# Where the split weights of a transformer block lie against the moving operands, and GpSimd's share of the gate and up projections on VectorE

## The chip, the cores and the metric

One core of a Trainium2 chip runs the whole kernel. The metric is the device time of one execution in microseconds. The kernel before was timed in three runs; their median is 2808.41 us (2807.86 to 2812.64). A further execution was taken under the profiler, and all rows of the trace are from that one.

## The reference

One encoder layer over 512 tokens of width 2048, in fp32: two attention mixers whose outputs are gated and merged, then a SwiGLU block of width 5632. What the change touches stands in the last lines:

```python
merged = jax.nn.sigmoid(ga) * (ya @ w_oa[l]) + jax.nn.sigmoid(gb) * (yb @ w_ob[l])
x = x + g1 * (merged @ w_out[l])

h2 = rms_norm(x, norm2_w[l]) * (1.0 + sc2) + sh2
ff = (jax.nn.silu(h2 @ w_ffn_gate[l]) * (h2 @ w_ffn_up[l])) @ w_ffn_down[l]
x = x + g2 * ff
return rms_norm(x, final_w)
```

## The kernel before, in words

**Three matmuls for one.** TensorE gets every fp32 operand as a pair: `split` (L113 to L115) copies a source to a high part on ACT (L114) and subtracts that from the source to a low part, on DVE unless told otherwise (L115). `mm3` (L122 to L124) then issues three matmuls into one bank: high by high, and the two mixed products. In `mm3(o, lh, ll, rh, rl)` the first pair is stationary (loaded as weights), the second pair moves past it.

**Tiles of split weights.** `wsplit` loads 512 KB of a weight matrix into a `raw` tile (DMA issued on SP) and splits it into a `whi` and a `wlo` tile, which `wtile` hands out. From `w_out` on, the pool has five buffers of each; each buffer has 1024 elements and 64 more, so that a tile can begin up to 63 elements (of 4 bytes) into its buffer. Where it begins is `wbufs["at"]` at the moment of the call. All buffers, and all tiles of split activations (`x`, `f`, `m`), begin at multiples of 256 bytes, and columns are taken from them in steps of 512 bytes; so `at` alone sets how a stationary and a moving operand lie against each other within 256 bytes.

**w_out.** `form2` keeps the activations stationary (`m`) and moves the weights, 512 columns a matmul, through four banks for the four blocks of 128 tokens; it is called for columns 0, 1, 2 with `at` 28, 44, 12, and for the last 512 columns in two halves, still at 12. Generators that compute the modulation vectors run between its steps (`pump`). After that `at` is 0.

**Gate and up.** `h2_unit` makes the normalised activations transposed, and `xforms` splits them into tiles `x0` to `x3` of each of four units of 512 rows. The first 512 columns of gate (n = 0) are computed plainly while these are made: weights stationary, 256 columns moving, one of the four moving blocks (`h21`) being itself a `wtile`. Everything else goes through `group7`, one call for up of n = 0 and then one each for gate and up of n = 1 to 10: 21 calls. It uses a Strassen-like scheme with seven products (forms 1, 2, 3, 5, 6, 7, 4, in this order) in place of eight, and takes four units of 84 matmuls each, all with weights stationary and 256 columns moving. For each unit `wforms` loads two raw tiles, forms two sums in `ta` on DVE (L705, L706) and two in `tb` on GpSimd (L707, L708), and splits four sources: a block of 512, a raw tile, `ta` and `tb`. At the end of a call seven operations (L765 to L771) combine the banks on DVE; the banks of forms 1, 2, 3, 5 are the four `mm` banks, which the next call overwrites in the same order. Before each call `at` takes the next value of `at7`: 4, 8, 12, 16, 20 and so on by fours to 60, then 0, 1, 2, 56, 24, 40.

**The product and down.** After up of each n, gate times up is formed (L840), on GpSimd but for the last n, and stored to DRAM (`ffd`). Down reads these back: `FF` loads half a stored tile (1024 wide, `ffr`), and splits it into `f0`, `f1` and so on, the first time a column pass asks for it; these tiles lie where the `x` tiles were. `form2` runs for four column blocks over the first five n and four over the next five (`at` 4, 8, 16, 24 and 32, 40, 48, 60), 240 matmuls of 512 columns in each, with `f` stationary and the weights moving. The last n stays in a tail with its own weight tiles, which begin at multiples of 256 bytes.

**Order.** The program is recorded in the order of the Python code, with some blocks at high priority, and a scheduler places each engine's instructions by priority; the engines execute them in that order and wait by semaphores.

Of the kernel before, what the change touches and what calls it, by code (L numbers as in the profile page):

```python
# [80 lines left out]
def encoder_block(ctx: ExitStack, tc, xp, c, w_ada, b_ada, norm1_w, w_in, q_norm_w, k_norm_w, tb,  # L81
                  w_oa, w_ob, w_out, norm2_w, w_gate, w_up, w_down, final_w, rope, wmask, out):
    nc = tc.nc
    V, S, G = nc.vector, nc.scalar, nc.gpsimd
# [9 lines left out]
    wbufs = {"raw": 4, "w": 3, "pad": 0, "at": 0}  # L94

    def wtile(tag):
        at = wbufs["at"]
        return wp.tile([P, 1024 + wbufs["pad"]], F32R, tag=tag, name=tag, bufs=wbufs["w"])[:, at:at + 1024]
    dram = ctx.enter_context(tc.tile_pool(name="dram", bufs=1, space=bass.MemoryType.DRAM))

    def bank(tag):
        return ps.tile([P, 512], F32, tag=tag, name=tag, bufs={"mm": 4, "S": 2, "T": 1, "Y": 1}[tag])
# [10 lines left out]
    def split(hi, lo, src, eng=V):  # L113
        S.activation(hi, src, AF.Copy)  # L114
        eng.tensor_sub(lo, src, hi)  # L115
# [10 lines left out]
    def unit(w, k0, nk, c0, ncol):  # L126
        raw = wp.tile([P, 1024], F32, tag="raw", name="raw", bufs=wbufs["raw"])
        r3 = raw[:, :nk * ncol].rearrange("p (k n) -> p k n", k=nk)
        nc.sync.dma_start(r3, w[k0 * P:(k0 + nk) * P, c0:c0 + ncol].rearrange("(k p) n -> p k n", p=P))
        return raw[:, :nk * ncol], r3  # L130
# [215 lines left out]
    for n, (k0, k1) in enumerate(slices):  # L346
# [9 lines left out]
        for k in ks:  # L356
            for i in range(NT):
                sl = slice(i * P, (i + 1) * P)
                nc.tensor.matmul(kv_b[i], hT[k][0][:, sl], hi[:, k - k0], start=k == 0, stop=False)
                nc.tensor.matmul(kv_b[i], hT[k][0][:, sl], lo[:, k - k0], start=False, stop=False)  # L360
        for k in ks:
            for i in range(NT):
                sl = slice(i * P, (i + 1) * P)
# [6 lines left out]
        for c0, accs, ends in ((QA, q_acc, (0, 1, 2, 4, 8, 12, 16)), (GA, g_acc, (0, 2, 6, 10, 14, 16))):  # L370
# [8 lines left out]
            for i, acc in enumerate(accs):  # L379
                sl = slice(i * P, (i + 1) * P)  # L380
# [270 lines left out]
        return evac  # L651

    for cc in range(3):
        wbufs["at"] = (28, 44, 12)[cc]
        form2(w_out, cc * 512, mT, residual(cc, gate, sq2, G, x2_d))
    for pr in ((0, 1), (2, 3)):
        form2(w_out, 3 * 512, mT, lambda i, b: residual(3, gate, sq2, V if i % 2 else G, x2_d)(i, b), tiles=pr)
        for i in pr:
# [5 lines left out]
            else:  # L664
                V.tensor_scalar(lo3, lo3, r, None, op0=ALU.mult)
                V.tensor_scalar(n3[i], hi1, r, None, op0=ALU.mult)
    wbufs["at"] = 0
    while bg:
        pump()
    p_m.release()  # L670
# [24 lines left out]
    def wforms(w, k0, c0):  # L695
        rt = []
        for a in range(2):
            raw, r3 = unit(w, k0 + 2 * a, 2, c0, 512)
            rt.append((raw, r3[:, :, :256], r3[:, :, 256:]))
        (_, b11, b12), (r1, b21, b22) = rt  # L700
        ta = wp.tile([P, 1024], F32, tag="ta", name="ta", bufs=2)
        tb = wp.tile([P, 1024], F32, tag="tb", name="tb", bufs=1)
        t1, t2_ = (half(ta)[:, a] for a in range(2))
        t3, t4 = (half(tb)[:, a] for a in range(2))
        V.tensor_sub(t1, b12, b11)  # L705
        V.tensor_sub(t2_, b22, t1)  # L706
        G.tensor_sub(t3, b22, b12)  # L707
        G.tensor_sub(t4, t2_, b21)  # L708
        hl = [[wtile(t) for t in ("whi", "wlo")] for _ in range(4)]
        col = lambda e: lambda t: t.rearrange("p (q n) -> p q n", q=2)[:, :, e * 256:(e + 1) * 256]  # L710
        blk = lambda e: lambda t: half(t)[:, e]
        g0 = [t[:, :512].rearrange("p (q n) -> p q n", q=2) for t in hl[0]]
        return split7(((b11, (lambda t: t,)), (r1, (col(0), col(1))), (ta, (blk(0), blk(1))), (tb, (blk(0), blk(1)))),
                      [g0] + hl[1:], HALVES[0])

    def xforms(pool, e, o, full=False):

        sa = wp.tile([P, 1024], F32, tag="ta", name="sa", bufs=2)
        sb = wp.tile([P, 1024], F32, tag="tb", name="sb", bufs=1)
        a11, a21 = e[:, :512], e[:, 512:]  # L720
        a12, a22 = o[:, :512], o[:, 512:]
        V.tensor_add(sa[:, :512], a21, a22)
        V.tensor_sub(sa[:, 512:], sa[:, :512], a11)
        G.tensor_sub(sb[:, :512], a11, a21)
        G.tensor_sub(sb[:, 512:], a12, sa[:, 512:])
        tl = [[pool.tile([P, 512 if n == 0 else 1024], F32R, tag=f"x{n}{t}", name=f"x{n}{t}") for t in "hl"]
              for n in range(4)]
        blk = lambda n: lambda t: t[:, n * 512:(n + 1) * 512].rearrange("p (q n) -> p q n", q=2)
        d = {}
        if full:  # L730
            h21 = [wtile(t)[:, :512] for t in ("whi", "wlo")]
            split(*tl[0], a11)
            split(*h21, a21)
            split(*tl[1], o)
            d["21"] = tuple(blk(0)(t) for t in h21)
            for n, rs in ((0, (1,)), (1, (2, 4))):
                for j, r in enumerate(rs):
                    d[r] = tuple(blk(j)(t) for t in tl[n])
            d.update(split7(((sa, (blk(0), blk(1))), (sb, (blk(0), blk(1)))), tl[2:], HALVES[1][2:]))
            return d  # L740
        return split7(((a11, (blk(0),)), (o, (blk(0), blk(1))), (sa, (blk(0), blk(1))), (sb, (blk(0), blk(1)))),
                      tl, HALVES[1])

    at7 = iter((4, 8, 12, 16, 20, 24, 28, 32, 36, 40, 44, 48, 52, 56, 60, 0, 1, 2, 56, 24, 40))

    def group7(wsrc, xs, order, dst):

        wbufs["at"] = next(at7)
        bk = {r: bank(BANK[r]) for r in ORDER}
        for n, s in enumerate(order):  # L750
            w = wsrc(s)
            for r in ORDER:
                (wh, wl), (xh, xl) = w[r], xs[s][r]
                for q in range(2):
                    for c in range(2):
                        o = bk[r][:, c * 256:(c + 1) * 256]
                        cs = slice(c * P, (c + 1) * P)
                        first, last = n == 0 and q == 0 and c == 0, n == len(order) - 1 and q == 1
                        mm3(o, wh[:, q, cs], wl[:, q, cs], xh[:, q], xl[:, q], first, last, skip_group_check=True)
        p = {r: b.rearrange("p (c n) -> p c n", c=2) for r, b in bk.items()}  # L760
        (d11, d12), (d21, d22) = dst
        with tc.high_priority():
            p1 = io.tile([P, 512], F32, tag="io", name="p1").rearrange("p (c n) -> p c n", c=2)
            S.activation(p1, p[1], AF.Copy)
            V.tensor_add(d11, p[2], p1)  # L765
            V.tensor_add(d21, p[6], p1)
            V.tensor_add(d12, p[5], d21)
            V.tensor_add(d12, p[3], d12)
            V.tensor_add(d21, p[7], d21)
            V.tensor_add(d22, p[5], d21)  # L770
            V.tensor_sub(d21, d21, p[4])  # L771

    SU = KT // 4
    FU = FT // 4
    f_x = [form_pool(f"f{n}", "left") for n in range(3)]

    def raw_tile(name):
        return wp.tile([P, 1024], F32, tag="raw", name=name, bufs=wbufs["raw"])
# [16 lines left out]
    hx = {}  # L795
    ff_d = [dram.tile([P, 2048], F32, name=f"ffd{n}") for n in range(FU)]
# [24 lines left out]
    def c_tile():  # L821
        c = c_p.tile([P, 2048], F32, tag="c", name="c", bufs=3)
        return c, c.rearrange("p (a t q n) -> p a t q n", a=2, t=2, q=2)

    for n in range(FU):
        cs = []
        for w in (w_gate, w_up):
            c, v = c_tile()
            cs.append(c)
            if n == 0 and w is w_gate:  # L830
                for f in range(4):
                    S.activation(v[:, f // 2, :, f % 2], banks[f].rearrange("p (t n) -> p t n", t=2), AF.Silu)
                continue
            dst = (v[:, 0, 0], v[:, 1, 0]), (v[:, 0, 1], v[:, 1, 1])
            group7(lambda s: wforms(w, 4 * s, n * 512), hx, range(SU), dst)
            if w is w_gate:
                S.activation(c, c, AF.Silu)
        for a in range(2):
            sl = slice(a * 1024, (a + 1) * 1024)
            (G if n < FU - 1 else V).tensor_mul(cs[1][:, sl], cs[1][:, sl], cs[0][:, sl])  # L840
        (nc.sync if n < FU - 1 else nc.scalar).dma_start(ff_d[n], cs[1])
    c_p.release()
    f3.release()
# [27 lines left out]
    class FF:  # L871
# [6 lines left out]

        def __getitem__(self, k):
            j, q = divmod(k, 2)  # L880
            if j not in self.pairs:
                n, a = divmod(j, 2)
                raw = raw_tile("ffr")
                nc.sync.dma_start(raw, ff_d[self.u0 + n][:, a * 1024:(a + 1) * 1024])
                hl = [self.pool.tile([P, 1024], F32R, tag=f"f{j}{t}", name=f"f{j}{t}") for t in "hl"]
                split(*hl, raw)
                self.pairs[j] = hl
            return tuple(Tokens(half(t)[:, :, q]) for t in self.pairs[j])

    for u0 in (0, 5):  # L890
        xs = FF(p_f, u0, 5)
        for cc in range(4):
            wbufs["at"] = (4, 8, 16, 24)[cc] if u0 == 0 else (32, 40, 48, 60)[cc]
            form2(w_down, cc * 512, xs, lambda i, b: residual(cc, g2, None, G)(i, b), r0=4 * u0)
    xs = FF(p_fl, 10, 1)
    xs = [xs[k] for k in range(4)]
# [9 lines left out]
    for cc in range(4):  # L906
        hi, lo = pair(p_l, f"w{cc}", 4 * 512, 1)
        for k in range(0, 4, 2):
            raw, _ = unit(w_down, f0 + k, 2, cc * 512, 512)
            sl = slice(k * 512, (k + 2) * 512)  # L910
            split(hi[:, sl], lo[:, sl], raw)
        wl.append((hi, lo))
    for i in range(NT):
        sl = slice(i * P, (i + 1) * P)
# [8 lines left out]
        for cc in range(4):  # L923
            cs = slice(cc * 512, (cc + 1) * 512)
# [36 lines left out]
```

## Time and profile before

| | us |
|---|---|
| median of 3 runs | 2808.41 |
| span of the profiled execution | 2800.4 |
| w_out | 1175 to 1367 |
| first gate block and its activations | 1367 to 1448 |
| 21 calls of `group7` | 1448.0 to 2281.8 |
| down and the tail | 2289.5 to the end |

The profiled execution has no time of its own beside its span; the runs, taken without the profiler, lie 8.0 us above it. In a row of the view of windows stand the stretch, its length, and each engine's busy time with its count of instructions, then the granted clock of TensorE, the share of the DMA engines and GB/s. PEld is the loading of weights. In a row of the timeline stand start, duration, engine, line, operation, and in brackets the idle time before it and what ended it.

### The profile page before, as it was taken

Reading aid. Unit: us, or ns where it says so; the run is one execution under the profiler, and the core shown is the slowest. Engines: PE = TensorE matmul, PEld = TensorE weight load, DVE = VectorE, ACT = ScalarE, POOL = GpSimd, SP = SyncE. Lnnn points to the kernel's source line nnn. Section 1 sums busy time; section 2 is a strip of 40 time slices with the busy share of each in tenths; the row PEclk is TensorE's granted clock in tenths of the full one; section 3 lists DMA queues with packets and bytes.
Section 4 is the critical chain, followed back from the end, with each engine's and each line's share of the span. In section 5 each row is a group of like instructions: output and inputs, shape, how many; then the busy total and the mean of one; then the engine's idle time right before and its main releaser. Section 6 shows DMA issues by size and latency. Waiting matters only on the chain.

```text
span 2800.4 us, 38853 instructions
## 1 busy us (share of the span) xinstructions
PE 2672.3 (95%) x15353; PEld 2331.3 (83%) x15353; DVE 1730.4 (62%) x2277; ACT 961.7 (34%) x1310; POOL 617.0 (22%) x366
## 2 busy tenths in 40 slices
PE   5888999999999999899899999999999989999998
PEld 4676878788887878677789999999999988878886
DVE  8987461566665566565568877777788753243227
ACT  4224441233331233222544444444444433122122
POOL 2544323000100000011123443333434410011000
PEclk8889999999999999999989999999999999999999
DMA  8772224655556577676333343334333354343232
GB/s 256 255 235 83 83 68 153 193 157 168 173 168 198 186 254 249 221 260 199 95 113 121 122 128 118 116 108 130 126 119 120 125 192 163 97 143 120 90 113 83
DMA packets 281238, 427.17 MB, mean 153 GB/s; under 512 B 16992, under 2 KB 148432, under 8 KB 278496
## 3 DMA queue, kind: packets, MB, share of 16 engines
q1 hardware_dynamic: 280720, 423.59, 46.9%
q8 instruction: 120, 1.97, 0.3%
q10 hardware_dynamic: 336, 1.11, 0.1%
q14 instruction: 62, 0.51, 0.1%
HBM read 392.11 MB, written 32.52 MB: 152 GB/s over the span
## 4 chain that ended last, share of the span: by engine, by line
PE 77%; DVE 10%; DMA 8%; ACT 2%; issue 2%; SPq 0%; POOL 0%; DVEq 0%; ACTq 0%
PE mm L122 19%; PE mm L124 19%; PE mm L123 19%; DMA raw<-in_w_ada 6%; DVE acc L257 5%; PE S L122 3%; PE S L123 3%; PE S L124 3%; PE Y L122 2%; PE Y L123 2%; PE Y L124 2%; DMA ffr<-ffd 1%; ACT whi L114 1%; PE T L494 1%; DVE wlo L115 0%
## 5 line engine op out<-in xcount | busy, mean ns | idle before, releaser
L114 ACT ACTIVATE whi<-raw 128x1024 fp32r<-128x1024 f32 (+1 forms) x466 | 455.2, 978 | 1077.0 <-PE mm L124 404.8
L115 DVE TENSOR_TENSOR wlo<-raw,whi 128x1024 fp32r<-128x1024 f32 (+1 forms) x408 | 499.4, 1227 | 494.6 <-ACT whi L114 489.7
L257 DVE SCALAR_TENSOR_TENSOR acc<-raw,cact,acc 128x512 f32<-128x512 f32 (+1 forms) x383 | 324.9, 851 | 138.0 <-DMA raw<-in_w_ada 129.0
L707 POOL TENSOR_TENSOR tb<-raw 128x512 f32<-128x512 f32 x84 | 116.0, 1380 | 505.6 <-DVE wlo L115 497.8
L115 POOL TENSOR_TENSOR wlo<-raw,whi 128x1024 fp32r<-128x1024 f32 (+1 forms) x58 | 142.7, 2465 | 236.5 <-ACT whi L114 204.9
L115 DVE TENSOR_TENSOR wlo<-ta,whi 128x1024 fp32r<-128x1024 f32 x84 | 129.4, 1541 | 70.5 <-ACT whi L114 70.1
L708 POOL TENSOR_TENSOR tb<-ta,raw 128x512 f32<-128x512 f32 x84 | 145.1, 1727 | 0.0
L646 POOL TENSOR_TENSOR xr<-xr,ro 128x512 f32<-128x512 f32 x32 | 49.3, 1572 | 434.0 <-DVE ro L645 434.0
L114 ACT ACTIVATE whi<-ta 128x1024 fp32r<-128x1024 f32 x84 | 89.2, 1062 | 142.1 <-PE mm L123 142.1
L114 ACT ACTIVATE whi<-tb 128x1024 fp32r<-128x1024 f32 x84 | 89.1, 1061 | 133.4 <-PE S L123 119.9
L123 PE MATMUL mm<-x1l,whi 128*128 128x256 f32 x400 | 112.4, 281 | 0.0
L122 PE MATMUL mm<-x1h,whi 128*128 128x256 f32 x400 | 112.3, 281 | 0.0
L124 PE MATMUL mm<-x1h,wlo 128*128 128x256 f32 x400 | 112.3, 281 | 0.0
L115 DVE TENSOR_TENSOR wlo<-tb,whi 128x1024 fp32r<-128x1024 f32 x84 | 102.5, 1221 | 10.0 <-ACT whi L114 8.3
L122 PE MATMUL mm<-x0h,whi 128*128 128x256 f32 x368 | 104.5, 285 | 3.3 <-ACT whi L114 3.3
L124 PE MATMUL mm<-x0h,wlo 128*128 128x256 f32 x368 | 104.4, 284 | 0.8 <-DVE wlo L115 0.8
L123 PE MATMUL mm<-x0l,whi 128*128 128x256 f32 x368 | 104.5, 284 | 0.0
L250 POOL MEMSET acc<- 128x512 f32 x8 | 4.2, 526 | 427.9 <-DVE ada_s L115 158.6
L123 PE MATMUL mm<-x3l,whi 128*128 128x256 f32 x336 | 94.3, 281 | 0.0
L123 PE MATMUL S<-x2l,whi 128*128 128x256 f32 x336 | 94.3, 281 | 0.0
L123 PE MATMUL S<-x3l,whi 128*128 128x256 f32 x336 | 94.3, 281 | 0.0
L123 PE MATMUL mm<-x2l,whi 128*128 128x256 f32 x336 | 94.3, 281 | 0.0
(1311 smaller groups left out, 8242.9 us busy)
## 6 DMA issues: line engine op xcount, KB each, us to landing
raw<-in_w_in SPq DMA_DIRECT2D x134, 512.0 KB
raw<-in_w_ada SPq DMA_DIRECT2D x256, 256.0 KB
raw<-in_w_gate SPq DMA_DIRECT2D x88, 512.0 KB
raw<-in_w_up SPq DMA_DIRECT2D x88, 512.0 KB
raw<-in_w_down SPq DMA_DIRECT2D x88, 512.0 KB
raw<-in_w_ada SPq DMA_DIRECT2D x64, 512.0 KB
raw<-in_w_out SPq DMA_DIRECT2D x40, 512.0 KB
ffr<-ffd SPq DMA_DIRECT2D x22, 512.0 KB
```

The lines of the kernel that those rows point to most:

```text
L114: S.activation(hi, src, AF.Copy)
L115: eng.tensor_sub(lo, src, hi)
L122: nc.tensor.matmul(o, lh, rh, start=start, stop=False, **kw)
L123: nc.tensor.matmul(o, lh, rl, start=False, stop=False, **kw)
L124: nc.tensor.matmul(o, ll, rh, start=False, stop=stop, **kw)
L250: G.memset(acc, 0.0)
L257: V.scalar_tensor_tensor(acc, part, cact[:, k:k + 1], acc, op0=ALU.mult, op1=ALU.add)
L494: nc.tensor.transpose(tp[:, k * P:(k + 1) * P], e[:, k * P:(k + 1) * P], ident)
L646: eng.tensor_add(x2[i][:, cs], x2[i][:, cs], o)
L707: G.tensor_sub(t3, b22, b12)
L708: G.tensor_sub(t4, t2_, b21)
```

## The change

It does four things. The offsets of `w_out` and of down become 0, and that of all of gate and up 16 elements (64 bytes), with `h21`, which moves, kept at 0. The two `tb` sums of `wforms` and all products of gate and up go from GpSimd to VectorE. During the last unit of the last `group7` call `first_pair` loads and splits the first half tile of `ffd` into a `whi`/`wlo` pair at offset 0, which down takes as its pair 0 in the first half (in `xforms` and the tail nothing else changes).

```diff
     for cc in range(3):
-        wbufs["at"] = (28, 44, 12)[cc]
         form2(w_out, cc * 512, mT, residual(cc, gate, sq2, G, x2_d))
...
-    wbufs["at"] = 0
+    wbufs["at"] = 16
...
-        G.tensor_sub(t3, b22, b12)
-        G.tensor_sub(t4, t2_, b21)
+        V.tensor_sub(t3, b22, b12)
+        V.tensor_sub(t4, t2_, b21)
...
+            at, wbufs["at"] = wbufs["at"], 0
             h21 = [wtile(t)[:, :512] for t in ("whi", "wlo")]
+            wbufs["at"] = at
...
-    at7 = iter((4, 8, 12, 16, 20, 24, 28, 32, 36, 40, 44, 48, 52, 56, 60, 0, 1, 2, 56, 24, 40))
-
     def group7(wsrc, xs, order, dst):
 
-        wbufs["at"] = next(at7)
...
+    pair0 = []
+
+    def first_pair(s):
+        if s == SU - 1:
+            wbufs["at"] = 0
+            raw = raw_tile("ffr")
+            nc.sync.dma_start(raw, ff_d[0][:, :1024])
+            pair0.extend((wtile("whi"), wtile("wlo")))
+            split(*pair0, raw)
+
...
-            group7(lambda s: wforms(w, 4 * s, n * 512), hx, range(SU), dst)
+            src = lambda s: wforms(w, 4 * s, n * 512)
+            if n == FU - 1 and w is w_up:
+                src = lambda s: (wforms(w, 4 * s, n * 512), first_pair(s))[0]
+            group7(src, hx, range(SU), dst)
...
-            (G if n < FU - 1 else V).tensor_mul(cs[1][:, sl], cs[1][:, sl], cs[0][:, sl])
+            V.tensor_mul(cs[1][:, sl], cs[1][:, sl], cs[0][:, sl])
...
         def __getitem__(self, k):
             j, q = divmod(k, 2)
+            if j not in self.pairs and j == self.u0 == 0:
+                self.pairs[0] = pair0
...
         for cc in range(4):
-            wbufs["at"] = (4, 8, 16, 24)[cc] if u0 == 0 else (32, 40, 48, 60)[cc]
```

VectorE at the end of a call of `group7` and the start of the next, before the change (`c` is the call's result, `p` the copied bank of form 1, `mm`, `S` and `Y` are banks; L770 is the last to read form 5's bank):

```order
L766 TENSOR_TENSOR c<-S,p_12008 128x512
L115 TENSOR_TENSOR wlo<-tb,whi 128x1024
L767 TENSOR_TENSOR c<-mm,c 128x512
L768 TENSOR_TENSOR c<-mm,c 128x512
L769 TENSOR_TENSOR c<-S,c 128x512
L115 TENSOR_TENSOR wlo<-raw,whi 128x512
L770 TENSOR_TENSOR c<-mm,c 128x512
L115 TENSOR_TENSOR wlo<-raw,whi 128x1024
L771 TENSOR_TENSOR c<-c,Y 128x512
L115 TENSOR_TENSOR wlo<-ta,whi 128x1024
```

The same place after it, where the lines are two lower (L766 is now L764, L770 is L768) and the call is one of up:

```order
L764 TENSOR_TENSOR c<-S,p_12008 128x512
L115 TENSOR_TENSOR wlo<-tb,whi 128x1024
L765 TENSOR_TENSOR c<-mm,c 128x512
L706 TENSOR_TENSOR tb<-raw 128x512
L766 TENSOR_TENSOR c<-mm,c 128x512
L767 TENSOR_TENSOR c<-S,c 128x512
L707 TENSOR_TENSOR tb<-ta,raw 128x512
L768 TENSOR_TENSOR c<-mm,c 128x512
L115 TENSOR_TENSOR wlo<-raw,whi 128x512
L769 TENSOR_TENSOR c<-c,Y 128x512
L851 TENSOR_TENSOR c<-c 128x1024 x2
L115 TENSOR_TENSOR wlo<-raw,whi 128x1024
```

The two sums of `tb` now stand among the combining operations, ahead of the split that was there, and the product (L851) stands ahead of the next splits.

ACT at the end of the last call and the start of down, before (with buffer numbers; `whi<-raw` are splits of w_down from `whi_21220` on, `p1` is the copy of form 1's bank, `ffd10` the store of the last product):

```order
L114 ACTIVATE whi_21094<-tb_21083 128x1024
L114 ACTIVATE whi_21220<-raw_21218 128x1024
L114 ACTIVATE whi_21269<-raw_21267 128x1024
L764 ACTIVATE p1_21188<-mm_20741 128x512
L114 ACTIVATE whi_21305<-raw_21303 128x1024
L114 ACTIVATE whi_21341<-raw_21339 128x1024
L114 ACTIVATE whi_21377<-raw_21375 128x1024
L841 DMA ffd10_10903<-c_20740 128x2048
L114 ACTIVATE f0h_21226<-ffr_21224 128x1024
L114 ACTIVATE f1h_21275<-ffr_21273 128x1024
```

And after it, where `whi_21106` is `pair0`:

```order
L114 ACTIVATE whi_21094<-tb_21083 128x1024
L114 ACTIVATE whi_21106<-ffr_21104 128x1024
L114 ACTIVATE whi_21226<-raw_21224 128x1024
L762 ACTIVATE p1_21194<-mm_20741 128x512
L114 ACTIVATE whi_21269<-raw_21267 128x1024
L114 ACTIVATE whi_21305<-raw_21303 128x1024
L114 ACTIVATE whi_21341<-raw_21339 128x1024
L114 ACTIVATE whi_21377<-raw_21375 128x1024
L852 DMA ffd10_10903<-c_20740 128x2048
L114 ACTIVATE f1h_21275<-ffr_21273 128x1024
```

The first pair's split has moved from the end of this row of splits to its head, ahead of the five splits of w_down; the others keep their order, and `f1h` follows the fifth.

## The prediction

> **What bounds the kernel now.** First the page: busy shares, then the chain that ended last, by engine.
>
> ```profile
> span 2800.4 us, 38853 instructions
> PE 2672.3 (95%) x15353; PEld 2331.3 (83%) x15353; DVE 1730.4 (62%) x2277; ACT 961.7 (34%) x1310; POOL 617.0 (22%) x366
> PE 77%; DVE 10%; DMA 8%; ACT 2%; issue 2%; SPq 0%; POOL 0%; DVEq 0%; ACTq 0%
> ```
>
> TensorE is busy for 95% of the span and owns 77% of the chain, so what matters is how fast matmuls follow each other and where TensorE stands still. A matmul's own duration in the trace overlaps the next one and does not give the pace. I read the pace from the view of windows, which counts instructions in a stretch: I laid windows on whole calls of `group7`, 336 matmuls of 256 columns each; about two of those counted began before the window.
>
> ```profile
> core 0: us, PE busy (x) PEld busy (x) DVE busy (x) ACT busy (x) POOL busy (x), PEclk, DMA share, GB/s
> 1567.10:1605.20 38.10, 38.10 (x338) 38.10 (x337) 33.97 (x32) 15.81 (x17) 20.04 (x10) 1.00 0.44 139
> 2003.40:2043.70 40.30, 40.30 (x338) 40.30 (x337) 27.96 (x33) 17.55 (x18) 11.62 (x9) 1.00 0.34 105
> 2043.70:2084.00 40.30, 40.30 (x338) 40.30 (x337) 34.50 (x32) 15.74 (x17) 19.11 (x11) 1.00 0.40 131
> 1448.00:2241.60 793.60, 793.60 (x6722) 793.60 (x6722) 618.65 (x617) 332.26 (x351) 309.30 (x179) 1.00 0.38 120
> 2241.60:2281.80 40.20, 40.20 (x337) 40.20 (x336) 23.80 (x27) 17.98 (x18) 8.53 (x6) 1.00 0.37 117
> ```
>
> The work in the first three rows is the same, the granted clock is 1.00 in each, and TensorE never waits; yet the first takes 38.1 us (113.4 ns a matmul) and the others 40.3 (119.9). What differs is the entry of `at7`: the fourth call, the first row, has 16 elements (64 bytes); the fifteenth and sixteenth have 60 and 0. All 20 calls of the fourth row average 39.7 us (118.1 ns). So the address of the weights against the moving operand sets the pace, and this kernel has already run the value that the change gives to every call.
>
> **The change part by part.**
>
> *Calls of `group7`.* At 38.1 us each, 20 calls take 762.0 in place of 793.6, the last one 38.1 in place of 40.2: **33.7 us** gone. I take the fourth call as the rule, not as luck: its DVE and POOL had as much to do as the others'. The ends: 38.1 for all (33.7), or for none but the one, with the rest at their mean now (0).
>
> *512-column matmuls.* For offset 0 with 512 columns I looked for a stretch where no call shifts the tiles: `w_oa`/`w_ob`, ahead of `w_out`, the first row here. The last four are `w_out`'s columns, and down's two halves stand between; the row at 1429 is the first gate block.
>
> ```profile
> 1000.00:1050.00 50.00, 50.00 (x222) 1.00 0.78 250
> 1193.00:1229.70 36.70, 36.70 (x160) 1.00 0.84 290
> 1234.00:1275.80 41.80, 41.80 (x180) 1.00 0.65 210
> 1280.00:1322.30 42.30, 42.30 (x183) 1.00 0.64 199
> 1322.50:1367.20 44.70, 44.70 (x194) 1.00 0.48 153
> 1429.00:1445.00 16.00, 16.00 (x136) 1.00 0.51 164
> 2296.00:2515.00 219.00, 219.00 (x946) 1.00 0.45 152
> 2517.70:2741.60 223.90, 223.90 (x957) 1.00 0.32 104
> 2757.00:2788.00 31.00, 31.00 (x139) 1.00 0.27 94
> ```
>
> (Read by their times: four rows from 1193 are `w_out`, 2296 and 2517 down, 2757 the tail, whose weights lie at 0 with the same stationary `f` tiles as down.) With two taken off each count, the first row has 50.0/220 = 227 ns and the tail 31.0/137 = 226; `w_out` has 232 to 235, down 232 and 234. At 227, `w_out`'s 158+178+181+192 = 709 matmuls take 161.0 in place of 165.5: **4.5 us**. Down's 944 + 955 take 431.1 in place of 442.9: **11.8 us**. The lower end for both is 0, if offset 0 helps only where weights are not the moving operand; the tail's row speaks against that, and against a loss. In `w_out` DMA is up to 0.84 busy, but inside these windows TensorE never waits for a load, so a 2% faster TensorE is still fed.
>
> *First gate block.* 384 matmuls of 256 columns go from offset 0 to 64 bytes; `h21`, moved there, stays at 0. 16.0/134 = 119 ns to 113.4 would give 2.3; part of the block waits for transposes and runs at half clock, so **2.0** (0 to 2.3).
>
> *Start of down.* Here TensorE waits, by the timeline (start, duration, engine):
>
> ```profile
> 2281.81 0.28 PE L124 MATMUL Y<-x1h,wlo 128*128 128x256 f32 x1
> 2289.53 0.79 PE L122 MATMUL mm<-whi,f0h 128*128 128x512 f32 x1 [7.44 <-ACT f0h L114]
> 2295.93 0.40 PE L124 MATMUL mm<-whi,f0l 128*128 128x512 f32 x1
> 2286.74 1.06 ACT L114 ACTIVATE whi<-raw 128x1024 fp32r<-128x1024 f32 x1 [5.00 <-DMA raw<-in_w_down]
> 2288.42 1.06 ACT L114 ACTIVATE f0h<-ffr 128x1024 fp32r<-128x1024 f32 x1 [0.62 <-DVE c L840]
> 2517.64 0.50 PE L122 MATMUL mm<-whi,f0h 128*128 128x512 f32 x1 [1.54 <-DVE ro L645]
> ```
>
> 7.6 us of idleness, then 14 starts in 6.40 us where 14 x 0.227 = 3.2 would do (granted clock below): 10.8 lost. With `pair0` ready, down's first step of 24 matmuls (5.45 us) follows at once. Then `f1h` is late: by the order of ACT above, it stands behind five splits of w_down, the fifth of which, `whi_21377`, needs a buffer. Of five, `pair0` holds one and the first four splits the others, so it waits until step one ends at 5.45; 1.06 for it, 1.06 for `f1h` (two such rows above) gives 7.6, and `f1l`, behind the low half of `whi_21377` on DVE, about 9.1. The third matmul of step two needs `f1l`, so TensorE loses 9.1 - 5.9 = 3.2. Gain 10.8 - 3.2 = **7.6 us**. If the clock drops again, 3.2 of that goes; if nothing waits, it is 10.8. Windows behind the two waits, with the granted clock after the count:
>
> ```profile
> 2289.50:2295.90 6.40, 6.33 (x14) 0.51 0.95 310
> 2517.60:2524.00 6.40, 6.36 (x27) 1.00 0.53 165
> ```
>
> 7.6 us of idleness halved the clock, the 1.5 at 2517 did not; 2.2 lies nearer the second, so I take no drop. The Trainium skill (TensorE: Matmul & The Clock Gate, What's actually happening) has a free-running window of about 3.4 us for the drop; by it too a wait of 2.2 us cannot fill one, and the sum stays.
>
> *GpSimd's part on VectorE.* Two subtractions a unit, 84 units, and the product of gate and up now stand in DVE's queue. The group boundary at 1605.23 behind the fast call, DVE in order of time, and the matmul for which it counts:
>
> ```profile
> 1603.01 0.69 DVE L706 TENSOR_TENSOR ta<-raw,ta 128x512 f32<-128x512 f32 x1
> 1603.62 0.68 DVE L766 TENSOR_TENSOR c<-S,p 128x512 f32<-128x512 f32 x1
> 1604.22 1.21 DVE L115 TENSOR_TENSOR wlo<-tb,whi 128x1024 fp32r<-128x1024 f32 x1
> 1605.35 0.68 DVE L767 TENSOR_TENSOR c<-mm,c 128x512 f32<-128x512 f32 x1
> 1606.07 0.69 DVE L768 TENSOR_TENSOR c<-mm,c 128x512 f32<-128x512 f32 x1
> 1607.27 1.34 DVE L115 TENSOR_TENSOR wlo<-raw,whi 128x512 fp32r<-128x512 f32 x1
> 1608.54 0.68 DVE L770 TENSOR_TENSOR c<-mm,c 128x512 f32<-128x512 f32 x1
> 1609.50 0.28 PE L122 MATMUL mm<-x2h,whi 128*128 128x256 f32 x1
> ```
>
> L770 is the last reader of the bank that form 5 of the next call overwrites: it ends at 1609.22, the matmul is at 1609.50, 0.28 to spare. Now form 5 comes three sevenths of 9.53 us behind 1605.23, at 1609.31. DVE loses the split at 1607.27 ahead of L770 (1.27 to the next start) and gets two subtractions (0.61 each, 1603.01 to 1603.62), which also fill the gap of 0.12 between L767 and L768: L770 ends at about 1609.05, 0.26 to spare. No wait, but close.
>
> ```profile
> L115 DVE TENSOR_TENSOR wlo<-ta,whi 128x1024 fp32r<-128x1024 f32 x80 | 124.5, 1557 | 62.6 <-ACT whi L114 62.2
> L115 DVE TENSOR_TENSOR wlo<-ta,whi 128x1024 fp32r<-128x1024 f32 x2 | 2.5, 1226 | 3.3 <-ACT whi L114 3.3
> L115 DVE TENSOR_TENSOR wlo<-raw,whi 128x512 fp32r<-128x512 f32 x2 | 1.5, 728 | 2.4 <-ACT whi L114 2.4
> L840 DVE TENSOR_TENSOR c<-c 128x1024 f32<-128x1024 f32 x2 | 2.4, 1218 | 0.0
> DVE wlo L115 <- ACT whi L114: 177.2, 180, 1.7
> ```
>
> Groups of lines: the first over the calls, the next two from 2250 to 2272, where GpSimd does little. Beside GpSimd a split takes 1557, without it 1226. So a call costs DVE 4 x (4 x 0.69 + 0.73 + 3 x 1.23) + 7 x 0.68 = 33.5 us, and 2.4 more behind up: 35.9 of 38.1. The product delays the splits behind it: the second split of the next unit then ends some 8.6 us past the boundary and is needed at 9.53 + 1.36 = 10.9. I cost all this at nothing; its cover is that slack, and if it is gone TensorE waits at each of 20 boundaries. The store of `ffd` on SP now stands ahead of up's eight loads, waiting for DVE's product (about 7.5 us past the boundary); their buffers come free only later, so nothing is late.
>
> **Sum.** 33.7 + 4.5 + 11.8 + 2.0 + 7.6 = 59.6. Span 2800.4 - 59.6 = 2740.8; the median of the runs is 2808.4, 8.0 above the span, so **2749 us**.
>
> **Rivals.**
> 1. *The bank wait decides.* If DVE is later than I count by more than 0.26 us, form 5 waits at all 20 boundaries; 0.2 to 1 us each is 4 to 20: 2753 to 2769. For: the small slack. Against: the added operations are shorter than what they replace. 12%.
> 2. *64 bytes is not the cause*, or not under every phase: the other 20 calls keep 39.7 on the mean: 2749 + 33 = 2782. For: one call only. Entries that recur vary (24 and 56 come twice). Against: the lowest and steadiest pace of 21 was this one, and half of 227 is 113.5, the pace of 512 columns at its best. 8%.
> 3. *The offset does not matter.* TensorE's load of weights would not disturb the moving operand, and only the start of down is left: 2808.4 - 7.6 = 2801. Against: 38.1 beside 40.3 in like calls. 2%. The Trainium skill (TensorE: Matmul & The Clock Gate, Step-by-step: what each phase is for) says that loading the next weights takes no SBUF read bandwidth from the running matmul, which would make this the outcome; the trace disagrees. The same time would come out if the shift did not reach the tiles.
> 4. *Slower: DVE becomes the bound.* It now idles 177.2 us for ACT's splits, 8.4 a call. If these waits stay, a call takes 33.5 + 1.2 + 8.4 = 43.1 us in place of 38.1: 21 x 5.0 = 105, so 2749 + 105 = 2854. It is slower than before from about 41 us a call. Against: ACT waits for TensorE to free a buffer, so these waits shrink when DVE is late. 4%.
>
> **How the numbers follow.** Forecast 2743 to 2757: 74%; rivals 12, 8, 2, 4%. For 8 in 10 the range takes in most of rival 1: 2743 to 2765. Faster by over 0.2% (5.6 us, about what a measurement of this kernel can tell): 74 + 12 + 8 + 1 = 95%; same 1%, slower 4%.
>
> **What would show it.** Each `group7` call 38.1 us in the windows; `w_out` and down at 227 ns a matmul; the first `f1h` matmul some 2 us late and no wait at `pair0`; no TensorE wait on DVE at L768's place. Wrong would be calls of 39 or more with no wait (rival 2), or TensorE waiting for DVE inside the calls (1, 4).

## The result and the profile after

| | before | after |
|---|---|---|
| median, us (4 runs each, side by side) | 2810.10 | 2760.92 |
| lowest to highest | 2807.86 to 2812.64 | 2758.62 to 2763.27 |
| ratio, 95% interval | | 0.9826 (0.9810 to 0.9841) |
| span of the profiled execution | 2800.4 | 2756.6 |

The changed kernel is 49 us faster; 59 were forecast, from 2808 to 2749. The page after, its span, busy shares and chain:

```profile
span 2756.6 us, 38761 instructions
PE 2627.7 (95%) x15353; PEld 2298.7 (83%) x15353; DVE 1758.6 (64%) x2465; ACT 961.2 (35%) x1310; POOL 290.4 (11%) x178
PE 80%; DVE 8%; DMA 7%; issue 2%; ACT 2%; SPq 0%; POOL 0%; DVEq 0%; ACTq 0%
```

TensorE is still the bound. GpSimd lost half of its work, and VectorE is busy for only 28 us more, because its own operations got shorter with less of GpSimd beside them. The splits of `ta` are one example: 84 of them took 1224 ns on the mean, where 80 had taken 1557:

```profile
L115 DVE TENSOR_TENSOR wlo<-ta,whi 128x1024 fp32r<-128x1024 f32 x84 | 102.9, 1224 | 70.6 <-ACT whi L114 70.5
```

The pace, from the view of windows of the changed kernel (stretch, length, TensorE's busy time and count, granted clock, DMA share, GB/s): the second column of `w_out`, the first gate block, all 21 calls, and down's two halves.

```profile
core 0: us, PE busy (x), PEclk, DMA share, GB/s
1242.00:1285.00 43.00, 43.00 (x191) 1.00 0.67 211
...
1437.00:1452.00 15.00, 15.00 (x135) 1.00 0.51 159
1453.50:2253.30 799.80, 799.80 (x7059) 1.00 0.41 125
2264.00:2475.60 211.60, 211.07 (x931) 1.00 0.48 158
2482.50:2697.90 215.40, 215.40 (x951) 1.00 0.34 105
```

Two off each count as in the prediction: the calls run at 799.8/7057 = 113.3 ns a matmul, all 21 of them in 38.08 us; `w_out` and down at 227 ns. That is the forecast pace in every stage. The timeline at the start of down:

```profile
2258.53 0.40 PE L124 MATMUL mm<-whi,wlo 128*128 128x512 f32 x1
2261.02 0.49 PE L122 MATMUL mm<-whi,f1h 128*128 128x512 f32 x1 [2.09 <-ACT f1h L114]
```

The first pair is there, and `f1h` is 2.26 us late (from 2258.53 + 0.23). The next wait, for `f1l`, costs 0.9: 3.2 us lost where 3.2 had been worked out.

Where the gain came short, the start of down's second half, by the same view:

```profile
2476.53 1.06 ACT L114 ACTIVATE f6h<-ffr 128x1024 fp32r<-128x1024 f32 x1 [4.45 <-DMA ffr<-ffd]
...
2477.62 1.23 DVE L115 TENSOR_TENSOR f6l<-ffr,f6h 128x1024 fp32r<-128x1024 f32 x1 [3.49 <-ACT f6h L114]
2478.76 1.88 DVE L645 TENSOR_TENSOR ro<-mm,g 128x512 f32<-128x512 f32 x3
...
2479.50 0.80 PE L122 MATMUL mm<-whi,f0h 128*128 128x512 f32 x1 [3.50 <-DVE ro L645]
```

TensorE needs banks that VectorE must empty (`ro`, L645). Those stand on VectorE behind `f6l`, a split for the second half, which waits for ScalarE's `f6h`, which waits for a load. From one matmul's start to the next it is now 3.89 us there; before, with the same chain, it was 1.94. The window behind the wait shows the granted clock at half:

```profile
2479.40:2482.30 2.90, 2.80 (x7) 0.50 0.53 181
```

Last, a part that the change doesn't touch: the first matmul of `w_out`, by the view of one tile (count, shortest, median and longest duration in ns, first and last start), before and then after.

```profile
L122 PE MATMUL mm<-whi,m0h x4: 388/448/628, 1175.4 to 1179.7; 128*128 128x512 f32 x4
```

```profile
L122 PE MATMUL mm<-whi,m0h x2: 629/711/793, 1184.0 to 1184.6; 128*128 128x512 f32 x2
```

Up to this place both kernels run the same instructions, yet the profiled execution of before got there 8.6 us earlier. So the spans differ by 43.8 us, while from `w_out` to the end the gain is 52.4.

### The profile page after: what moved, and what is told of

It reads as the page before. It is cut to its first block, busy times and chain, and to the rows that moved or that the text cites. A ratio compares the mean times of both kernels' runs of the same rounds, so it can differ in the third digit from the quotient of the medians.

```text
span 2756.6 us, 38761 instructions
## 1 busy us (share of the span) xinstructions
PE 2627.7 (95%) x15353; PEld 2298.7 (83%) x15353; DVE 1758.6 (64%) x2465; ACT 961.2 (35%) x1310; POOL 290.4 (11%) x178
## 4 chain that ended last, share of the span: by engine, by line
PE 80%; DVE 8%; DMA 7%; issue 2%; ACT 2%; SPq 0%; POOL 0%; DVEq 0%; ACTq 0%
PE mm L122 20%; PE mm L124 20%; PE mm L123 20%; DMA raw<-in_w_ada 4%; DVE acc L257 4%; PE S L122 4%; PE S L123 4%; PE S L124 4%; PE Y L122 2%; PE Y L123 2%; PE Y L124 2%; DMA ffr<-ffd 1%; PE Y L275 1%; PE mm L359 1%; PE T L494 1%
## 5 line engine op out<-in xcount | busy, mean ns | idle before, releaser
L115 DVE TENSOR_TENSOR wlo<-raw,whi 128x1024 fp32r<-128x1024 f32 (+1 forms) x408 | 457.7, 1125 | 390.1 <-ACT whi L114 384.8
L257 DVE SCALAR_TENSOR_TENSOR acc<-raw,cact,acc 128x512 f32<-128x512 f32 (+1 forms) x383 | 318.0, 833 | 163.0 <-DMA raw<-in_w_ada 155.6
L115 DVE TENSOR_TENSOR wlo<-ta,whi 128x1024 fp32r<-128x1024 f32 x84 | 102.9, 1224 | 70.6 <-ACT whi L114 70.5
L124 PE MATMUL mm<-x2h,wlo 128*128 128x256 f32 x336 | 92.9, 276 | 0.0
L124 PE MATMUL mm<-x3h,wlo 128*128 128x256 f32 x336 | 92.9, 276 | 0.0
L124 PE MATMUL S<-x2h,wlo 128*128 128x256 f32 x336 | 92.9, 276 | 0.0
L124 PE MATMUL Y<-x1h,wlo 128*128 128x256 f32 x336 | 92.9, 276 | 0.0
L124 PE MATMUL S<-x3h,wlo 128*128 128x256 f32 x336 | 92.9, 276 | 0.0
```

The lines of the kernel that those rows point to most:

```text
L124: nc.tensor.matmul(o, ll, rh, start=False, stop=stop, **kw)
L257: V.scalar_tensor_tensor(acc, part, cact[:, k:k + 1], acc, op0=ALU.mult, op1=ALU.add)
```

## The experiments

**The kernel before again**, unaltered, to see how much its profile scatters.

> The kernel before, profiled once more. In the two traces at hand the first matmul of w_out starts at 1175.4 us (before) and 1184.0 us (after), though every engine's program is the same up to there. Theory A: that is scatter of the executions, and the profiled one of before was a fast one. Then this trace has that matmul several us later than 1175.4 (1179 to 1186), and a span of 2803 to 2811. Theory B: the change delays the part ahead of it in a way that the program does not show. Then this trace is at 1175 again, with a span near 2800. In both the runs stand about 2 us above their spans. Ratio 1.00.

2809.74 us, ratio 0.9998 (0.9985 to 1.0011). Its `w_out` began at 1174.8, which by itself is what theory B had said. Against theory B stand the other runs: over the fourteen profiled executions of this study, all with the same instructions up to there, that start lay between 1174.8 and 1187.7, and the change, profiled again, had it at 1179.1 in place of 1184.0. The 25 executions of the kernel before that were timed beside it lie between 2797.52 and 2814.67 us, with a median of 2808.87, so one with a span of 2800.4 us is an early one. The 8.6 us are therefore put down to scatter. That the two profiles of the kernel before are the two earliest of the fourteen, and what makes the start vary, stayed open.

**The offsets alone.** The sums and products stay on GpSimd, and there is no early pair.

```diff
-        wbufs["at"] = (28, 44, 12)[cc]
...
-    wbufs["at"] = 0
+    wbufs["at"] = 16
...
-        wbufs["at"] = next(at7)
...
-            wbufs["at"] = (4, 8, 16, 24)[cc] if u0 == 0 else (32, 40, 48, 60)[cc]
```

> The change's offsets alone: tb's sums and the products stay on GpSimd, no first pair. Theory A (the address alone sets the pace, and GpSimd was no hindrance): calls of group7 at 38.1 us, w_out and down at 227 ns a matmul, start of down as before the change (10.8 us lost): some 42 us faster than before, ratio 0.985. Theory B (the faster pace needs the work off GpSimd, since the wait for form 5's bank had only 0.28 us to spare beside it): TensorE waits for DVE at the boundaries or inside the calls, calls of 38.5 us or more, 10 us or more of the gain missing, ratio 0.989 or above.

2793.22 us, ratio 0.9938 (0.9918 to 0.9957); all four executions between 2789 and 2797. This is a third of the gain, and the profile shows why. The windows from the end of the gate block over the first call to the start of the second, then over most of the second, and over the calls from there on:

```profile
1433.20:1494.40 61.20, 61.20 (x542) 1.00 0.41 122
1494.60:1533.40 38.80, 38.80 (x331) 1.00 0.44 136
...
1500.00:2280.00 780.00, 780.00 (x6625) 1.00 0.40 121
```

61.2/540 = 113.3 ns, then 38.8/329 and 780/6623 = 117.8: at one offset, one clock and one order, a second pace, 39.57 us a call, which holds for twenty calls without a wait. Between the two stands this, by the timeline of VectorE and of TensorE at the start of the second call:

```profile
1492.35 1.34 DVE L115 TENSOR_TENSOR wlo<-raw,whi 128x512 fp32r<-128x512 f32 x1
1493.61 0.68 DVE L768 TENSOR_TENSOR c<-mm,c 128x512 f32<-128x512 f32 x1
```

```profile
1494.26 0.28 PE L124 MATMUL mm<-x3h,wlo 128*128 128x256 f32 x1
1494.43 0.36 PE L122 MATMUL mm<-x2h,whi 128*128 128x256 f32 x1
1494.63 0.28 PE L123 MATMUL mm<-x2l,whi 128*128 128x256 f32 x1
1494.74 0.28 PE L124 MATMUL mm<-x2h,wlo 128*128 128x256 f32 x1
```

Form 5's first matmul starts 0.17 us behind the one ahead of it and the next 0.20, where 0.113 is the pace. I read this as a wait of about 0.14 us for L768, the last reader of form 5's bank, which ended at 1494.29 because a split beside GpSimd (1.34 us) stood ahead of it. The view names no cause for so short a wait; but the first matmul is lengthened to 0.36 us, as the first one is behind the forced waits further below (0.39). It is the place of rival 1. In the changed kernel the sums on VectorE have moved that split behind L768 (for the same place three calls on):

```profile
1608.93 0.68 DVE L768 TENSOR_TENSOR c<-mm,c 128x512 f32<-128x512 f32 x1
1609.54 0.68 DVE L115 TENSOR_TENSOR wlo<-raw,whi 128x512 fp32r<-128x512 f32 x1
```

```profile
1609.94 0.28 PE L122 MATMUL mm<-x2h,whi 128*128 128x256 f32 x1
```

L768 ends at 1609.61, 0.33 us ahead of the matmul, and the pace of 113.3 goes on.

**VectorE's part alone**, at the old offsets.

```diff
-        G.tensor_sub(t3, b22, b12)
-        G.tensor_sub(t4, t2_, b21)
+        V.tensor_sub(t3, b22, b12)
+        V.tensor_sub(t4, t2_, b21)
...
-            (G if n < FU - 1 else V).tensor_mul(cs[1][:, sl], cs[1][:, sl], cs[0][:, sl])
+            V.tensor_mul(cs[1][:, sl], cs[1][:, sl], cs[0][:, sl])
```

> The kernel before with tb's sums and the products on VectorE, offsets as before, no first pair. Theory A (it costs and brings nothing while TensorE is the bound): calls keep their lengths, 793.6 us for 20, ratio 1.00 within 0.2%. Theory B (DVE beside GpSimd was slow enough to matter): calls get shorter without any change of offset, 10 us or more, ratio below 0.997. Theory C (DVE too full): slower, ratio above 1.002. DVE's split of ta goes from 1.54 us to 1.23 in any case.

2810.72 us, ratio 1.0003 (0.9989 to 1.0018): nothing by itself. Each of its 21 calls is as long as before to 0.02 us.

**The early pair alone**: `first_pair` and `pair0`, with the old offsets otherwise.

> The kernel before with the first pair split ahead of down (at offset 0), everything else as before. Theory A: start of down loses 3 to 3.5 us (f1h late) in place of 10.8, nothing else changes: 7 to 8 us faster, ratio 0.997. Theory B (a faster start is given back at the next wait): down's later waits grow by as much, ratio 0.999 to 1.000.

2803.64 us, ratio 0.9981 (0.9969 to 0.9994): 5 us faster, between 2 and 9 by the interval, which holds the 7.6 that the profile shows at that place.

**One late call.** If one wait settles the pace, VectorE work put into one call should show it.

```diff
         V.tensor_sub(t4, t2_, b21)
+        for _ in range(late):
+            V.tensor_sub(t4, t2_, b21)
...
-            src = lambda s: wforms(w, 4 * s, n * 512)
+            src = lambda s: wforms(w, 4 * s, n * 512, 3 if n == 5 and w is w_gate and s < 2 else 0)
```

> The change, with three more identical VectorE subtractions in each of the first two units of one call, the tenth of 21 (3.6 us of VectorE work at 0.6 us each, there only). Theory A (one wait flips the pace of the calls for good, as the 0.14 us wait at the second call did in the run with the offsets alone): TensorE waits once at the start of call 9 or 10 (counted from 0), calls before it take 38.08 us, and all behind it 39.57 us: about 11 x 1.49 = 16 us above the change, some 2777 us. Theory B (a wait costs itself only; the slower pace of that run has to do with GpSimd sharing the memory with VectorE in every call): the calls behind it are at 38.08 us again, and the time stays within 3 us of the change's 2761. Theory C (a wait draws the pace anew among several values): calls behind it at a constant pace which is neither.

It didn't test that: TensorE waited nowhere in the calls of the profiled execution. But the four executions fell into two groups, 2755.92 and 2759.75 against 2789.61 and 2790.23 (ratio 0.9865, 0.9804 to 0.9927), 21 x 1.49 = 31 us apart, and the profiled one, of the second group, is at 117.8 ns from the first call on. So the pace had been settled ahead of the calls.

**Offsets exchanged**: gate and up at 0, `w_out` and down at 64 bytes.

```diff
+    wbufs["at"] = 16
...
-    wbufs["at"] = 16
+    wbufs["at"] = 0
...
+            wbufs["at"] = 16
```

> The change with its two offsets exchanged: gate's and up's weights at 0, those of w_out and down at 64 bytes (16 elements); order and work as in the change. If the offset sets the pace: the 21 calls take 40.3 us each as the call with entry 0 did before (21 x 2.2 = 46 us more), w_out and down lie at 229 to 232 ns a matmul in place of 227 (709 + 1899 matmuls x 2 to 5 ns = 5 to 13 us more): 2812 to 2820 us, no better than before. If the gain came from VectorE's part and the early pair, with the offset of no account: 2761 us.

2811.46 us, ratio 0.9997 (0.9985 to 1.0009), with VectorE's part and the early pair in it. Its windows, the 21 calls and down's halves:

```profile
1450.70:2297.40 846.70, 846.70 (x7058) 1.00 0.39 118
2310.00:2520.00 210.00, 210.00 (x914) 1.00 0.46 155
2531.00:2747.00 216.00, 216.00 (x945) 1.00 0.33 105
```

120.0 ns in the calls and 229 to 230 in down, as expected: the offset sets the pace, each way for its own shape. (The Trainium skill, TensorE: Matmul & The Clock Gate, Step-by-step: what each phase is for, says that loading weights costs the running matmul no read bandwidth. By that the exchange would have changed nothing; 38.1 beside 40.3 us for the same call disagrees.)

**The distance, not the address**: the `x` tiles 64 bytes on, the weights at 128.

```diff
-    wbufs["at"] = 16
+    wbufs["at"] = 32
...
-            at, wbufs["at"] = wbufs["at"], 0
+            at, wbufs["at"] = wbufs["at"], 16
...
+    gap_l = form_pool("gap_l", "left")
+    gap_l.tile([P, 16], F32, name="gap_l")
...
+                gap_r = form_pool("gap_r", "right")
+                gap_r.tile([P, 48], F32, name="gap_r")
...
```

> The change with the normalized x tiles of gate and up moved by 64 bytes (a spacer in their pools) and the weights at 128 bytes (32 elements) in place of 64: the distance between the two operands stays 64 bytes modulo 256. If the distance decides: calls at 38.08 us, time within 3 us of the change's. If the address of the weights alone decides: calls as with 32 elements against unmoved x in the kernel before, about 40 us, 21 x 2 = 42 us more, 2803 us.

2762.44 us, ratio 0.9836 (0.9790 to 0.9883): 2753.16, 2759.47, 2765.41, and the profiled execution at 2784.93. The three are the change's time, and not the 2803 of weights at 128 bytes against unmoved tiles: the distance between the operands decides. The profiled one shows where its slower pace began. Windows in the first gate block, between TensorE's stops for transposes, then at half clock, then the last stretch, which runs on into the calls:

```profile
1386.10:1394.10 8.00, 7.66 (x68) 1.00 0.40 126
1407.00:1417.00 10.00, 9.14 (x78) 1.00 0.35 110
1424.00:1426.80 2.80, 2.80 (x14) 0.50 0.82 253
1427.00:1447.00 20.00, 20.00 (x172) 1.00 0.55 171
```

By busy time the first stretch runs at 7.66/68 = 113 ns, the second at 9.14/78 = 117, the last at 20.0/170 = 118. So the pace can change where TensorE starts again. That the last such start, the return of the full clock ahead of the first call, settles what the calls inherit is seen in two other runs, where the pace changed just there. The last long stretch ahead of that return and the one behind it (between the two lie a stop for transposes and the half clock), first with the offsets alone, then in the last run of this section:

```profile
1413.00:1420.00 7.00, 7.00 (x62) 1.00 0.42 149
1434.00:1449.00 15.00, 15.00 (x135) 1.00 0.65 202
```

```profile
1409.50:1417.50 8.00, 8.00 (x73) 1.00 0.48 161
1430.00:1449.00 19.00, 19.00 (x164) 1.00 0.52 166
```

With two off each count, 117 ns becomes 113 in the one, and 113 becomes 117 in the other. In all nine profiled executions with 64 bytes in the calls, the pace behind that return is the pace of the first call.

**The change again**, in more executions.

> The change itself, unaltered. Theory A (with 64 bytes between the operands a stretch of matmuls runs at one of two paces, 113.3 or 117.8 ns; which one is drawn where TensorE's clock comes back ahead of the first call, and it then stays for all 21 calls): most executions at 2755 to 2766 us and some at about 2787 to 2797, nothing between, as in the runs with a late call and with the moved x tiles; from those, about 3 of 16. Theory B (the slow pace in those two runs came from their own edits): all executions at 2755 to 2766 us.

Ratio 0.9846 (0.9800 to 0.9891), and theory A: 2751.18, 2751.62, 2755.59, 2756.70, and 2785.09, 2792.27. The profiled one is of the second group, its calls in one window:

```profile
1448.80:2279.80 831.00, 831.00 (x7058) 1.00 0.40 120
```

831.0/7056 = 117.8 ns; from `w_out` to its end it is 31.3 us longer than the profile after, which is 21 x 1.49. Of ten executions of the change, eight lie at 2751 to 2763 us and two at 2785 to 2792. With the other five kernels of this study that have 64 bytes, VectorE's part and no wait in the calls, it is by their times 8 of 32 at the slower pace.

**An extra addition in each call**, to make TensorE wait at every boundary.

```diff
-            V.tensor_add(d11, p[2], p1)
+            for _ in range(next(again)):
+                V.tensor_add(d11, p[2], p1)
```

> The change with the first of the seven combining additions of every call of group7 done twice or three times, by turns (0.69 us of VectorE work each, ahead of the last readers of the banks; the additions repeat a value, nothing else changes). The spare 0.26 us is gone, so TensorE waits some 0.4 and 1.1 us by turns for L768 or L770's place at each of the 20 boundaries. Theory A (each wait draws the pace anew): calls lie at 38.08 or 39.57 us and change only at such waits, both values occur: 15 us of waits and up to 31 us of pace, 2776 to 2807 us. Theory B (a wait always leads to 117.8 ns, and no later wait leads back): every call behind the first wait at 39.57 us, 2761 + 15 + 30 = 2806 us. Theory C (waits cost themselves only): calls at 38.08 us and 2776 us.

A miss: 2754.92 us, ratio 0.9801 (0.9782 to 0.9819), no wait in the calls. This addition's bank is full well ahead of the boundary, so the repeats went into VectorE's idle time. It only says that VectorE has that much to spare there.

**A wait at each boundary**, with the addition that stands on the path to L768's read.

```diff
-            V.tensor_add(d12, p[5], d21)
+            for _ in range(2):
+                V.tensor_add(d12, p[5], d21)
```

> The change with the combining addition of L765, which stands ahead of the last readers of the banks of forms 3 and 5, done twice in every call (the repeat adds nothing to the result). On VectorE it and a split that now goes first put L768's last read of form 5's bank 1.2 us later, so it ends 0.95 us behind the start that TensorE has in the change: at each of the 20 boundaries TensorE waits about 0.5 us ahead of form 3 and as much ahead of form 5, 20 x 1.0 = 20 us in all. Theory A (each wait draws the pace of what follows anew): matmuls between waits lie at 113.3 in some calls and at 117.8 ns in others, 2774 to 2804 us. Theory B (a wait always leads to 117.8 ns, none leads back): 117.8 ns in all calls behind the first boundary, about 2804 us. Theory C (a wait costs itself alone): one pace in all calls, that of the first, 2776 us, or 2804 in executions which begin at 117.8 ns.

2773.30 us, ratio 0.9878 (0.9862 to 0.9895), all four executions at 2770 to 2776. One wait at each boundary, not two, since form 5 comes in time once form 3 has waited; 0.49 us from start to start at the third call's boundary, here by the timeline:

```profile
1528.79 0.28 PE L122 MATMUL S<-x2h,whi 128*128 128x256 f32 x1
1529.28 0.39 PE L122 MATMUL mm<-x3h,whi 128*128 128x256 f32 x1 [0.21 <-DVE c L767]
```

And windows inside four calls in a row, the ninth to the twelfth, clear of the waits:

```profile
1762.00:1795.00 33.00, 33.00 (x293) 1.00 0.42 128
1801.00:1835.00 34.00, 34.00 (x291) 1.00 0.50 155
1841.00:1874.00 33.00, 33.00 (x294) 1.00 0.45 129
1879.00:1912.00 33.00, 33.00 (x293) 1.00 0.51 160
```

113.4, 34.0/289 = 117.6, 113.0, 113.4 ns: one wait took the pace from 113.3 to 117.8 and the next brought it back. The same happened at the twentieth call and the one behind it; the other waits left it at 113.3. This fits theory A: the pace can change at a wait, and it can go both ways. Whether it is drawn by chance stayed open, since the two slow calls of this one profile lie exactly ten calls apart. In the run with the offsets alone the slower pace was a trap. At its next boundary, one call further on, form 5 comes late enough:

```profile
1532.94 0.68 DVE L768 TENSOR_TENSOR c<-mm,c 128x512 f32<-128x512 f32 x1
```

```profile
1534.08 0.28 PE L122 MATMUL mm<-x2h,whi 128*128 128x256 f32 x1
```

L768 ends at 1533.62, 0.46 us ahead of the matmul, so the wait of 0.14 us at which the pace could change again doesn't occur. That it is this which held all four executions there was read from one profile, not tried.

**Down's pairs beside the weights.** The wait at the second half, tried by loading the raw pairs into buffers that are idle by then.

```diff
-                raw = raw_tile("ffr")
+                raw = wp.tile([P, 1024], F32, tag="ta", name="ffr", bufs=2)
```

> The change with down's raw pairs loaded into the two buffers of ta, idle by then, in place of the raw buffers, which they share with w_down's loads. If the wait at the start of down's second half (3.9 us, and some 1.5 us of halved clock behind it) comes from VectorE's evacuations standing behind the low half of a pair that is late by its load, that wait falls to about 1.5 to 2 us and the clock stays up: 2 to 4 us less, 2757 us. If the load isn't what makes the pair late (ScalarE's and VectorE's own queues do), the wait stays and the time is within 1 us of the change's.

2764.84 us, ratio 0.9828 (0.9810 to 0.9846). That is not told apart from the change's 0.9826, where 4 us less were expected. The wait at the second half is gone; but in the first half the fourth pair came late, and TensorE stood for 10.8 us from start to start:

```profile
2285.96 1.06 ACT L114 ACTIVATE f3h<-ffr 128x1024 fp32r<-128x1024 f32 x1 [8.13 <-DMA ffr<-ffd]
```

**The second half's pairs alone.**

```diff
+                raw = wp.tile([P, 1024], F32, tag="ta", name="ffr", bufs=2) if self.u0 == 5 else raw_tile("ffr")
```

> The change with the raw pairs of down's second half alone loaded into the two buffers of ta; the first half's stay in the raw buffers, since with all of them moved the fourth pair came 10 us late. If both readings are right (the second half's wait goes, as it went with all pairs moved; the first half is as in the change): 3.9 us of wait and about 1.5 us of halved clock less, 2756 us. If the ring of loads or VectorE makes up for it: within 1 us of the change's, 2761.

Its six executions: 2746.29, 2748.68, 2750.63 at one pace and 2778.78, 2781.01, 2781.39 at the other; ratio 0.9842 (0.9799 to 0.9886). Its median, 2764.71, says little, since three of six had the slower pace. Pace by pace, beside the change in its six executions above, timed together with these, the means are 2748.5 against 2753.8 and 2780.4 against 2788.7: 5 and 8 us faster. All that TensorE waits for from the start of down on, by the view of waits (total, times, longest):

```profile
PE mm L123 <- DVE w0l L115: 2.3, 1, 2.3
PE mm L122 <- ACT f1h L114: 2.1, 1, 2.1
PE mm L124 <- DVE f1l L115: 0.7, 1, 0.7
```

The wait for `ro` is gone, which lasted 3.2 to 4.2 us in every profile with the change's down unaltered. (The wait for `f5l`, in the first half, is absent too, but it came and went without any change there: it is in the profile of the change again and not in that with the late call.) This is the best version found, as far as three executions at a pace can say.

## Why the prediction held, point by point

The 2760.92 us measured lie outside the 2743 to 2757 of the forecast itself. They are inside the stated 2743 to 2765 only by the part that was added for rival 1, whose waits did not occur; what filled that part is worked out below. That the time fell within the range was to this extent luck. So was it that all four executions had the faster pace: with 8 of 32 at the slower one, an estimate for four in a row is (24/32)^4, about one in three.

Measured from `w_out` to the end, so without the scatter ahead of it (in us; the row of down's pace is what the other three leave of the sum):

| term | forecast | measured |
|---|---|---|
| calls of `group7` | 33.7 | 34.0 |
| `w_out` and first gate block | 6.5 | 3.2 |
| start of down | 7.6 | 7.6 |
| down's pace | 11.8 | 7.6 |
| sum | 59.6 | 52.4 |

- **Calls, right in the profile and in 8 of 10 executions.** The pace was 113.3 ns in each of the 21 calls, so the fourth call had been a fair guide. In the other two executions the term is worth 833.8 - 831.0 = 2.8 us in place of 34. The prediction did not see that one offset has two paces; the one call that it took for the rule had been at the faster of them.
- **`w_out` and the gate block, mis-sized.** The pace was right. But in `w_out` a faster TensorE waited longer for banks that VectorE empties (`ro`, L645: 3.3 us in place of 1.6), and stretches at half clock gained nothing. From its first matmul to its last `w_out` took 190.1 us in place of 191.8, and the gate block gave 1.4: half of the term went.
- **Start of down, right in each part**: 2.26 us for `f1h`, 3.2 lost, no drop of the clock. The last was not safe, though: as the last section shows, an idle of the same 2.26 us at the tail was followed by a drop.
- **Down's pace, mis-sized.** 227 ns held. 2.0 us went into the longer wait at the second half, 1.2 into the halved clock behind it, 0.7 into a new wait for `f5l`. The prediction looked for what is late next only at the start of down; the run with the second half's pairs moved shows that the late load was the cause of the first of these; what made `f5l` late was not tried.
- **"I cost all this at nothing" of VectorE's part: right for the change, but for half a reason.** Alone it is worth nothing, as forecast. With the offsets it takes away the wait that led to the slower pace. Rival 1 named that wait and its place, and priced it at 0.2 to 1 us a boundary. Made to occur, it cost 0.5 us a boundary and a draw of the pace; where GpSimd caused it, it cost 1.49 us in every call.
- **The 8.0 us between span and median, mis-sized.** Each run lies some 2.0 us above its own span. The other 6 were the early profile of before. The change's span came out 15.8 us above the forecast 2740.8: 8.6 from ahead of `w_out` and 7.2 from the terms. With 2.0 outside the span, and 2.3 by which the median lies above the profiled run, in place of the 8.0, that makes the 12 us between 2749 and 2760.92.
- **Rivals 3 and 4 fell, and 2 in the main.** Exchanged offsets gave nothing, so the offset is the cause; VectorE never held TensorE up in the calls. But the sign of rival 2, calls of 39 us or more without a wait, did come in two of the ten executions, at 2785 and 2792 us where the rival had said 2782. What it left out is that this happens at 64 bytes, in every call of such an execution.

## What to carry to other kernels

Where TensorE never waits, read its pace as a count over a stretch, and try the distance between stationary and moving operands within 256 bytes, for each shape of matmul by itself. Then take away the small waits too, since behind one wait of 0.14 us each call took 1.49 us more. Time such a kernel often enough to see whether its executions fall into two groups, and compare group with group.

## What the runs showed of the hardware

- At 64 bytes between the operands, 256 columns run at 113.3 or at 117.8 ns a matmul, and stay there until TensorE next stops. At 0 they ran at 120.0, in every call of the profiled execution with the offsets exchanged. With the old offsets each of the 21 calls kept its own pace, the same to 0.03 ns in four executions of three kernels. But two calls with one and the same offset could differ there: with 24 elements one took 39.88 us and another 39.43. Why a call at an old offset never changed from one execution to the next, and why the distance matters at all, stayed open.
- With 512 columns it is the other way round: 227 ns at 0 and 229 to 230 at 64 bytes.
- The granted clock fell to 0.56 behind an idle of 2.26 us at the start of the tail, and stayed at 1.00 behind one of 2.17 at the same place before:

```profile
2700.56 0.57 PE L123 MATMUL mm<-w0l,f0h 128*128 128x512 f32 x1 [2.26 <-DVE w0l L115]
```

```profile
2700.50:2703.30 2.80, 2.74 (x7) 0.56 0.53 154
```

The Trainium skill (TensorE: Matmul & The Clock Gate, What's actually happening) has idle windows of some 3.4 us for this; by that a wait of 2.26 could not have done it, and the trace disagrees.
